# Seven products for half of the state space's output product and for a third gate/up pair

## The chip, the cores and the metric

One core of a Trainium2 chip runs the kernel. The metric is the device time of one execution in microseconds (us); lower is better. Engines are named as in the profile: PE (TensorE matmuls), PEld (its weight loads, which run beside them), DVE (VectorE), ACT (ScalarE), POOL (GpSimd) and SP (SyncE, which issues most loads). L12 is line 12 of the kernel.

## What is computed

Two layers of a decoder trunk on 256 tokens of width 1024, in float32. In each layer, after an RMSNorm, one wide input product feeds a retention mixer and a state-space mixer; each has its own output product, the two results are gated and added, and `w_o` brings them back. A SwiGLU block follows. Only the lines that matter here:

```
    ys = (ysg.reshape(bsz, s, SSD_INNER) * ssd_norm_w.astype(jnp.float32)).astype(h.dtype)
    o_ssd = ys @ ssd_out                                   # (256 x 2048) @ (2048 x 1024)
    merged = jax.nn.sigmoid(gate_ret) * o_ret + jax.nn.sigmoid(gate_ssd) * o_ssd
    return merged @ w_o
...
    gu = h @ w_gate_up                                     # (256 x 1024) @ (1024 x 5632)
    gate, up = jnp.split(gu, [D_FF], axis=-1)
    return (jax.nn.silu(gate) * up) @ w_down               # (256 x 2816) @ (2816 x 1024)
```

## The kernel before, in words

**Precision.** Every float32 operand is split into two float32r parts, high (`wh`) and low (`wl`). A product of 128 rows by 512 columns is three matmuls: high by high, low by high, high by low (`mm3`, L535 to L538). A weight piece is 128 by 1024 numbers (512 KB): SP loads it into a `raw` slot (4 of them), ACT writes `wh` (L499), DVE subtracts to get `wl` (L520). `split_piece` takes one of `HB` = 6 slots for the pair (`hlS`); the matmuls that use it last give it back. Pieces are split in the order in which the products use them (`turn`).

**Three ways to do a product.** *Plain* (`tm_job`, `out_job`): four tiles of 128 tokens by 512 columns. For a gate/up pair of 512 columns each this is 96 matmuls of 512 columns and 8 split pieces. *Feature-major* (`fm_job`, L957 to L960): the weights are stationary, high and low tokens stand side by side, so that a step is one matmul of 512 columns and one of 256; a pair has eight blocks of eight steps and 8 pieces. Its result comes out transposed, as the down product wants it; two PSUM halves have to be added (`gathered`). *Seven products* (`sevens`, `wino_sums`, `seven`): Strassen's scheme in Winograd's form. Tokens and the inner dimension are halved, the pair's two column blocks are the other halves, and seven block products (named 11, t1, t2, 22, t3, 21, t4) of 12 matmuls each take the place of eight: 84 matmuls of 512 columns. For that, the weights have sums: t1 = 11 + 12 and t2 are added by DVE in place (two pieces each), t3 and t4 by a DMA that adds while it writes (`accum_op`, issued by POOL, four in all), and all seven sums have to be split: 14 pieces. The operands have sums too (`seven_sums`: on each of four sums one DVE addition, an ACT copy and a DVE subtraction), and four DVE operations put the products together.

**Buffers of a seven.** The two pieces of 11, which become t1, t2 and t4 in place, lie in the slots of `seg`; those of 12, which become t3, in the two `cc` slots; 22 and 21 in `raw`.

**Where each stands.** In every layer: the mixer's input products (one pair by sevens), `ret`, four jobs `z`, `ssd` (plain, 16 pieces), `wo`, then the feed-forward block `FFN`: pair 0 plain, 1 feature-major, 2 seven, 3 feature-major, 4 seven, and half a pair (index 5) feature-major. The down product (`out_wino`) does 1024 of its 2816 rows (parts 1 and 2 of its operand `gu`) by sevens, mixed into 14 plain pieces by the pattern `AMID`, where "*" is a plain piece and the last five pieces stand behind the pattern.

**What sets the order.** A planner inside the kernel (`Flow`) plays the streams with costs of its own and writes down each engine's instructions in the order that comes out; the engines then run them in that order and wait on semaphores. SP's loads stand in the order of the products' pieces (`feeder`), each behind a free slot.

## Time and profile before

| | |
|---|---|
| median of 3 runs | 1263.66 us (1262.74 to 1264.23) |
| the profiled execution | 1261.89 us, span of its instructions 1260.1 us |
| PE busy | 1251.6 us, 99% of the span, 6330 matmuls |
| DVE busy | 1017.9 us, 81% |
| ACT busy | 832.7 us, 66% |
| POOL busy | 52.6 us, 4% |
| DMA | 253.96 MB, 202 GB/s on average |

A row's "mean ns of one" is longer than the step from one instruction to the next, since neighbours overlap in their pipelines; the step is read from two starts in the timeline. "Idle before" names what ended the wait.

### The profile page before, as it was taken

The numbers are of one execution on the slowest core, as the hardware profiler recorded it, in microseconds if no ns is written. First come the engines' busy times: TensorE is split into PE (matmuls) and PEld (weight loads), VectorE is DVE, ScalarE is ACT, GpSimd is POOL, SyncE is SP. The second block draws the span as 40 slices with busy tenths as digits, with TensorE's granted clock in tenths as the row PEclk, the third lists the DMA queues.
The fourth block names the chain that finished last, engine by engine and source line by source line (L and its number), as shares of the span: only waits on it lengthen the run. The fifth ranks groups of instructions, "written<-read, shape, count | busy, mean of one in ns | idle before, by whom it ended". The sixth has DMA issues, their size and how long they took to land.

```text
span 1260.1 us, 17460 instructions
## 1 busy us (share of the span) xinstructions
PE 1251.6 (99%) x6330; PEld 1061.8 (84%) x6330; DVE 1017.9 (81%) x1388; ACT 832.7 (66%) x1245; POOL 52.6 (4%) x76
## 2 busy tenths in 40 slices
PE   9999999999999999999999999999999999999997
PEld 8889888888888888888888898888888888888886
DVE  6998978878575678999788888878875756888996
ACT  6866786987365466776586676967954643766754
POOL 0000000000010001001000000000000000010010
PEclk9999999999999999999999999999999999999999
DMA  8768555556465557987777475555555664678873
GB/s 298 226 175 276 189 168 174 166 194 196 155 218 201 163 174 224 294 228 206 225 217 220 123 260 175 172 186 169 189 193 176 201 207 151 211 217 257 281 190 114
DMA packets 72456, 253.96 MB, mean 202 GB/s; under 512 B 8337, under 2 KB 8593, under 8 KB 72369
## 3 DMA queue, kind: packets, MB, share of 16 engines
q1 hardware_dynamic: 66832, 233.32, 55.8%
q0 software_dynamic: 5248, 18.99, 7.9%
q8 instruction: 50, 0.82, 0.3%
q10 hardware_dynamic: 288, 0.52, 0.1%
q14 instruction: 38, 0.30, 0.1%
HBM read 251.69 MB, written 1.11 MB: 201 GB/s over the span
## 4 chain that ended last, share of the span: by engine, by line
PE 95%; DVE 2%; DMA 1%; issue 1%; ACT 0%; POOLq 0%; POOL 0%; ACTq 0%
PE acc L536 20%; PE acc L537 20%; PE acc L538 20%; PE acc L957 16%; PE acc L958 9%; PE tr L633 2%; PE acc L960 2%; PE yps L1616 2%; DVE wl L520 1%; DMA raw<-in_w_dw_dram 1%; PE tr L1509 1%; PE acc L1376 1%; PE ips L1603 1%; PE idle L1949 0%; PE y L537 0%
## 5 line engine op out<-in xcount | busy, mean ns | idle before, releaser
L520 DVE TENSOR_TENSOR wl<-raw,wh 128x1024 fp32r<-128x1024 f32 (+2 forms) x400 | 475.4, 1197 | 111.1 <-ACT wh L499 108.9
L499 ACT ACTIVATE wh<-raw 128x1024 fp32r<-128x1024 f32 (+2 forms) x400 | 409.5, 1037 | 214.8 <-PE acc L538 108.7
L957 PE MATMUL acc<-xT,wh 128*128 128x512 f32 x840 | 304.2, 400 | 0.0
L958 PE MATMUL acc<-xT,wl 128*128 128x256 f32 x960 | 252.7, 282 | 0.0
L536 PE MATMUL acc<-wh,xT 128*128 128x512 f32 (+1 forms) x568 | 219.7, 387 | 0.0
L538 PE MATMUL acc<-wh,xT 128*128 128x512 f32 (+1 forms) x568 | 216.3, 381 | 0.0
L537 PE MATMUL acc<-wl,xT 128*128 128x512 f32 (+1 forms) x568 | 216.2, 381 | 0.0
L958 PEld LDWEIGHTS acc<-xT,wl 128*128 128x128 f32 x960 | 181.7, 189 | 10.0
L957 PEld LDWEIGHTS acc<-xT,wh 128*128 128x128 f32 x840 | 158.3, 188 | 32.1
L537 PEld LDWEIGHTS acc<-wl,xT 128*128 128x128 f32 x568 | 106.8, 188 | 20.0 <-issue 1.0
L536 PEld LDWEIGHTS acc<-wh,xT 128*128 128x128 f32 x568 | 106.8, 188 | 19.5 <-issue 1.4
L538 PEld LDWEIGHTS acc<-wh,xT 128*128 128x128 f32 x568 | 106.8, 188 | 19.4
L499 ACT ACTIVATE wh<-raws 128x1024 fp32r<-128x1024 f32 x64 | 67.2, 1056 | 29.7 <-DVE raws L228 14.5
L520 DVE TENSOR_TENSOR wl<-raws,wh 128x1024 fp32r<-128x1024 f32 x64 | 77.4, 1222 | 9.3 <-ACT wh L499 9.1
L231 DVE SCALAR_TENSOR_TENSOR cc<-cc,cv 128x255 f32<-128x255 f32 (+1 forms) x144 | 68.9, 480 | 11.5 <-ACT cc L221 10.4
L536 PE MATMUL acc<-wh,A 128*128 128x512 f32 x192 | 76.4, 398 | 0.0
L538 PE MATMUL acc<-wh,A 128*128 128x512 f32 x192 | 74.9, 390 | 0.0
L537 PE MATMUL acc<-wl,A 128*128 128x512 f32 x192 | 74.8, 390 | 0.0
L536 PE MATMUL acc<-wh,C 128*128 128x512 f32 (+1 forms) x184 | 72.3, 393 | 0.0
L537 PE MATMUL acc<-wl,C 128*128 128x512 f32 (+1 forms) x184 | 71.0, 386 | 0.0
L538 PE MATMUL acc<-wh,C 128*128 128x512 f32 (+1 forms) x184 | 70.8, 385 | 0.0
L536 PE MATMUL acc<-wh,Y 128*128 128x512 f32 x160 | 64.3, 402 | 0.0
(176 smaller groups left out, 1853.4 us busy)
## 6 DMA issues: line engine op xcount, KB each, us to landing
raw<-in_w_tm_dram SPq DMA_DIRECT2D x104, 512.0 KB, 4.3
raw<-in_w_fm_dram SPq DMA_DIRECT2D x80, 512.0 KB, 4.2
raw<-in_w_gf_dram SPq DMA_DIRECT2D x40, 512.0 KB, 4.8
raw<-in_ret_out_dram SPq DMA_DIRECT2D x32, 512.0 KB, 3.9
raw<-in_ssd_out_dram SPq DMA_DIRECT2D x32, 512.0 KB, 3.4
raw<-in_w_gate_up_dram SPq DMA_DIRECT2D x32, 512.0 KB, 5.4
raw<-in_w_down_dram SPq DMA_DIRECT2D x28, 512.0 KB, 4.5
raw<-in_w_gr_dram SPq DMA_DIRECT2D x24, 352.0 KB, 3.9
```

What stands on the lines that cost most here:

```text
L231: return Op("dve", 1.04 * n + 130, lambda: nc.vector.scalar_tensor_tensor(out=out, in0=in0, scalar=scalar, in1=in1, op0=op0, op1=op1), pr)
L499: nc.scalar.activation(out=wh[:, :m], in_=raw[:, :m], func=AF.Copy)
L520: nc.vector.tensor_tensor(out=wl[:, :m], in0=raw[:, :m], in1=wh[:, :m].bitcast(F32), op=ALU.subtract)
L536: nc.tensor.matmul(ps, lhsT=lh, rhs=rh, start=first, stop=False, **kw)
L537: nc.tensor.matmul(ps, lhsT=lh, rhs=rl, start=False, stop=False, **kw)
L538: nc.tensor.matmul(ps, lhsT=ll, rhs=rh, start=False, stop=last, **kw)
L633: nc.tensor.transpose(out=ps[:, j * P : (j + 1) * P], in_=src[:, j * P : (j + 1) * P], identity=ident)
L957: nc.tensor.matmul(a, lhsT=wh[:, k % 4, fsl], rhs=x[:, k % 4, :, :], start=k == 0, stop=False)
L958: nc.tensor.matmul(a[:, :SEQ], lhsT=wl[:, k % 4, fsl], rhs=xh[:, k % 4, :], start=False, stop=False)
L960: nc.tensor.matmul(a, lhsT=wh[:, k % 4, fsl], rhs=x[:, k % 4, :, :], start=False, stop=True)
L1376: nc.tensor.matmul(ps[:, :SEQ], lhsT=k[:, b, :P], rhs=q[:, b, :], start=b == 0, stop=b == 1)
L1616: nc.tensor.matmul(ps[:, i * HD : (i + 1) * HD], lhsT=sg[:, i, :], rhs=xdt[:, i * HD : (i + 1) * HD], start=True, stop=True)
```

## The change

- **Output product of the state space.** Its first 1024 rows (parts 0 and 1 of the operand `yz`) go by sevens, the other 1024 stay plain (8 pieces): `out_wino` is used here too, with a pattern `SMID` of its own, a new weight layout `w_sw`, and `add_m`, which gates the seven's results and adds them to the sum `sgr`. The operand's sums start with job `z` 2.
- **Feed-forward.** Pair 1 goes by sevens in place of feature-major, pair 2 feature-major in place of sevens; pair 3 goes by sevens, and the half pair 5 moves ahead of pair 4, which stays seven and is now last. So three pairs go by sevens and one and a half feature-major.
- **Down product.** In `AMID` six plain pieces, where there were four, stand ahead of the first product; the count is the same.
- **Slots.** `HB` 7 for 6: a seventh pair of `wh` and `wl`. `dynamic_dma_scratch_size` is set to 8192, half of what it was.
- **`seven_sums`** waits for all four parts of its operand before it takes buffers.

```diff
-GF = (1, 3, NPAIR)
+GF = (2, NPAIR)
...
-    HB, RB, TAIL, WARM = 6, 4, 5, 2
+    HB, RB, TAIL, WARM = 7, 4, 5, 2
...
+    ZS_PR = 0.5
...
-    AMID = ("*", "*", "*", "*", "11", "*", "t1", "*", "t2", "22", "*", "t3", "*", "21", "*", "t4")
+    AMID = ("*", "*", "*", "*", "*", "*", "11", "*", "t1", "*", "t2", "22", "*", "t3", "21", "t4")
+
+    SMID = ("*", "*", "11", "*", "t1", "*", "t2", "22", "*", "t3", "21", "t4")
...
         for n in range(2):
             for t in range(NT):
+                yield (plain[n][t] if plain else op.ready[parts[n]][t])
+        for n in range(2):
+            for t in range(NT):
                 if plain:
                     x[n, t] = yield plain[n][t]
                 else:
-                    yield op.ready[parts[n]][t]
...
     FFN = [[("plain", 0)],
-           [("fm", 1)],
-           [("seven", (2,), ("t3", "t4"))],
-           [("fm", 3)],
-           [("seven", (4,), ("t3", "t4"))],
-           [("fm", NPAIR)]]
+           [("seven", (1,), ("t3", "t4"))],
+           [("fm", 2)],
+           [("seven", (3,), ("t3", "t4"))],
+           [("fm", NPAIR)],
+           [("seven", (4,), ("t3", "t4"))]]
...
-            if isinstance(m, tuple):
+            if m == ("ssd",):
+                group(sevens(w_sw[l, 0], w_sw[l, 1], added=("t3", "t4"), order=SMID, slots=(ccS, new_cc)),
+                      plain((out_srcs(ssd_out[l])[8:], ())))
+            elif isinstance(m, tuple):
...
+            if g == 2:
+                fl.spawn(seven_sums(zops, yz, (0, 1), "A", at_job[0] + ZS_PR))
             return tm_job(xT, z_post(g))
...
+        def add_m(t, n, u, j):
+            nsl = slice(n * 512, (n + 1) * 512)
+            yield sgs_ev[t][n]
+            yield mr_ev[t][n]
+            inner = (t, n) == (1, 0)
+            if inner:
+                yield sxS
+            to = new_sx() if inner else u
+            yield tt(512, j, to, u, sgs[t][:, nsl], ALU.mult)
+            yield tt(512, j, sgr[t][:, nsl], sgr[t][:, nsl], to, ALU.add)
+            if inner:
+                fl.release(sxS)
+
+        zops = {q: Event() for q in ALONE}
...
-            return out_job(yz, 16, ssd_post)
+            return out_wino(yz, 16, 0, "A", SMID, ssd_post, add_m, zops)
...
+    out["w_sw"] = cols(a["ssd_out"][:, :1024], [0, 512], 512, 2)
...
-    nc = _bacc.Bacc("TRN2", target_bir_lowering=False, num_devices=1)
+    nc = _bacc.Bacc("TRN2", target_bir_lowering=False, num_devices=1, dynamic_dma_scratch_size=8192)
```

How the instructions stand before and after, at three places. DVE in layer 1, around the end of the plain pair 0. `wl` is a split's subtraction, `raws<-raws,cc` and `raws<-raws,raw` are the additions of t1 and t2, `plain` and `D` the operand's sums. Before:

```order
L520 TENSOR_TENSOR wl<-raw,wh 128x1024
L228 TENSOR_TENSOR D<-plain,D 128x4x128
L520 TENSOR_TENSOR wl<-raw,wh 128x1024
L228 TENSOR_TENSOR plain<-plain 128x512
L520 TENSOR_TENSOR wl<-raw,wh 128x1024
L228 TENSOR_TENSOR D<-plain,D 128x4x128
L520 TENSOR_TENSOR wl<-raw,wh 128x1024
L228 TENSOR_TENSOR plain<-plain 128x512
L520 TENSOR_TENSOR wl<-raw,wh 128x1024 x2
L228 TENSOR_TENSOR D<-plain,D 128x4x128
L228 TENSOR_TENSOR sil<-acc,sil 128x512 x2
```

After, up to the second t2 piece:

```order
L523 TENSOR_TENSOR wl<-raws,wh 128x1024
L229 TENSOR_TENSOR D<-plain,D 128x4x128
L523 TENSOR_TENSOR wl<-raws,wh 128x1024
L229 TENSOR_TENSOR plain<-plain 128x512
L229 TENSOR_TENSOR raws<-raws,cc 128x1024
L229 TENSOR_TENSOR D<-plain,D 128x4x128
L229 TENSOR_TENSOR raws<-raws,raw 128x1024
L229 TENSOR_TENSOR sil<-acc,sil 128x512 x2
L523 TENSOR_TENSOR wl<-raws,wh 128x1024 x2
L229 TENSOR_TENSOR raws<-raws,raw 128x1024
L229 TENSOR_TENSOR A<-tr,A 128x4x128 x2
L523 TENSOR_TENSOR wl<-raw,wh 128x1024
```

In the place of plain splits for a feature-major pair there are now the additions and splits of a seven, among the operand's sums. SP's loads from `wo` to the down product. Before:

```order
L481 DMA raw<-in_w_o_dram 128x1024 x8
L481 DMA raw<-in_w_gate_up_dram 128x1024 x8
L481 DMA raw<-in_w_gf_dram 128x1024 x8
L481 DMA raws<-in_w_gate_up_dram 128x1024 x2
L481 DMA cc<-in_w_gate_up_dram 128x1024 x2
L481 DMA raw<-in_w_gate_up_dram 128x1024 x4
L481 DMA raw<-in_w_gf_dram 128x1024 x8
```

After:

```order
L484 DMA raw<-in_w_o_dram 128x1024 x8
L484 DMA raw<-in_w_gate_up_dram 128x1024 x8
L484 DMA raws<-in_w_gate_up_dram 128x1024 x2
L484 DMA cc<-in_w_gate_up_dram 128x1024 x2
L484 DMA raw<-in_w_gate_up_dram 128x1024 x4
L484 DMA raw<-in_w_gf_dram 128x1024 x8
```

The first seven's eight loads now stand directly behind the eight of the plain pair. POOL between the state space's norm weights and the down product (`rz` and `rstd` are small powers for norms). Before:

```order
L661 DMA wb<-in_norm_ffn_w_dram 128x1024
L241 TENSOR_TENSOR rstd<-ms,mhalf 128x1 x2
L409 DMA cc<-in_w_gate_up_dram 128x1024 x2
L409 DMA raws<-in_w_gate_up_dram 128x1024 x2
L409 DMA cc<-in_w_gate_up_dram 128x1024 x2
L409 DMA raws<-in_w_gate_up_dram 128x1024 x2
L661 DMA wb<-in_norm_mix_w_dram 128x1024
```

After:

```order
L412 DMA cc<-in_w_sw_dram 128x1024
L242 TENSOR_TENSOR rz<-ms,mhalf 128x1
L412 DMA cc<-in_w_sw_dram 128x1024
L242 TENSOR_TENSOR rz<-ms,mhalf 128x1
L664 DMA wb<-in_norm_ffn_w_dram 128x1024
L412 DMA raws<-in_w_sw_dram 128x1024 x2
L242 TENSOR_TENSOR rstd<-ms,mhalf 128x1 x2
L412 DMA cc<-in_w_gate_up_dram 128x1024 x2
L412 DMA raws<-in_w_gate_up_dram 128x1024 x2
```

Adding DMAs stand now between the norm powers of the last `z` job, and there is one more group of four in the feed-forward block. Over the whole program PE has 16 transposes, 144 matmuls of 512 columns more in the plain form (L536 to L538) and 128 fewer of each size in the feature-major form; DVE has 40 operations of 1024 columns (24 splits, 16 additions) and 52 of 512 more, and 16 of 256 fewer; ACT 24 splits more; POOL 16 adding DMAs more (28 before); SP as many loads as before.

## Rows read from the trace of the kernel before

**Rows 1.** The page of the profile: the span, the engines' busy time, PE's share and granted clock in 40 slices, and the first line of the chain that ended last.

```profile
span 1260.1 us, 17460 instructions
PE 1251.6 (99%) x6330; PEld 1061.8 (84%) x6330; DVE 1017.9 (81%) x1388; ACT 832.7 (66%) x1245; POOL 52.6 (4%) x76
...
PE   9999999999999999999999999999999999999997
...
PEclk9999999999999999999999999999999999999999
...
PE 95%; DVE 2%; DMA 1%; issue 1%; ACT 0%; POOLq 0%; POOL 0%; ACTq 0%
```

**Rows 2.** Busy time of each engine in stretches of 10 us of layer 1's feed-forward block; the last two columns are the DMA engines' busy share and GB/s.

```profile
core 0: us, PE busy (x) PEld busy (x) DVE busy (x) ACT busy (x) POOL busy (x), PEclk, DMA share, GB/s
480.00:490.00 10.00, 10.00 (x60) 8.72 (x59) 6.59 (x9) 5.69 (x8) 0.00 (x0) 1.00 0.88 354
490.00:500.00 10.00, 10.00 (x57) 8.64 (x56) 10.00 (x12) 6.50 (x10) 1.80 (x2) 1.00 0.63 106
500.00:510.00 10.00, 10.00 (x45) 8.29 (x45) 10.00 (x12) 8.79 (x11) 1.72 (x2) 1.00 0.80 184
510.00:520.00 10.00, 10.00 (x49) 8.37 (x48) 10.00 (x13) 7.93 (x10) 0.00 (x0) 1.00 0.78 250
...
540.00:550.00 10.00, 10.00 (x47) 8.35 (x46) 10.00 (x12) 8.95 (x11) 2.28 (x3) 1.00 0.74 135
```

**Rows 3.** Timeline of PE in layer 1, from the feature-major pair 1 to the seven of pair 2 and into pair 3 (start in us, busy us, line, operation).

```profile
484.58 0.40 PE L957 MATMUL acc<-xT,wh 128*128 128x512 f32 x1
...
498.68 0.40 PE L536 MATMUL acc<-wh,xT 128*128 128x512 f32 x1
...
501.42 0.39 PE L536 MATMUL acc<-wh,D 128*128 128x512 f32 x1
...
512.30 0.39 PE L536 MATMUL acc<-wh,xT 128*128 128x512 f32 x1
```

**Rows 4.** The chain of waits, one step of it: PE's eight transposes of two tiles.

```profile
458.88 0.87 PE tr L633 x8
```

**Rows 5.** Timeline of DVE through the seven of pair 2 in layer 1; a bracket, where there is one, is idle time ahead of the row.

```profile
500.33 1.22 DVE L520 TENSOR_TENSOR wl<-raws,wh 128x1024 fp32r<-128x1024 f32 x1
...
502.07 2.36 DVE L520 TENSOR_TENSOR wl<-raw,wh 128x1024 fp32r<-128x1024 f32 x2
504.34 0.69 DVE L228 TENSOR_TENSOR C<-sil,C 128x512 fp32r<-128x512 f32 x1
504.94 2.36 DVE L520 TENSOR_TENSOR wl<-cc,wh 128x1024 fp32r<-128x1024 f32 x2
507.22 1.22 DVE L520 TENSOR_TENSOR wl<-raw,wh 128x1024 fp32r<-128x1024 f32 x1
```

**Rows 6.** Timeline of DVE in layer 1 behind the norm, during the plain pair 0, and in the feature-major pair 1.

```profile
464.54 2.35 DVE L520 TENSOR_TENSOR wl<-raw,wh 128x1024 fp32r<-128x1024 f32 x2
...
478.98 0.69 DVE L228 TENSOR_TENSOR A<-tr,A 128x512 fp32r<-128x512 f32 x1 [0.37 <-ACT A L221]
479.58 0.41 DVE L228 TENSOR_TENSOR sil<-acc,sil 128x256 f32<-128x256 f32 x1
479.91 0.68 DVE L228 TENSOR_TENSOR A<-tr,A 128x512 fp32r<-128x512 f32 x1
481.58 1.22 DVE L520 TENSOR_TENSOR wl<-raw,wh 128x1024 fp32r<-128x1024 f32 x1 [0.98 <-ACT wh L499]
```

**Rows 7.** Busy time of each engine over layer 1's feed-forward block up to the down product; columns as in rows 2.

```profile
452.00:572.00 120.00, 120.00 (x619) 102.28 (x617) 108.91 (x129) 87.21 (x117) 8.06 (x10) 1.00 0.81 248
```

**Rows 8.** Timeline of PE in layer 1: the first matmul of the plain pair 0.

```profile
452.59 0.39 PE L536 MATMUL acc<-wh,xT 128*128 128x512 f32 x1
```

**Rows 9.** Timeline of SP's loads in layer 1: those of the plain pair 0, then of pair 1.

```profile
433.88 22.32 SPq L481 DMA_DIRECT2D raw<-in_w_gate_up_dram  x8
457.35 11.64 SPq L481 DMA_DIRECT2D raw<-in_w_gf_dram  x5
```

**Rows 10.** The page's DMA issues: operation, count, KB each, median us from issue to landing.

```profile
raws<-in_w_gate_up_dram SPq DMA_DIRECT2D x8, 512.0 KB, 7.0
cc<-in_w_gate_up_dram SPq DMA_DIRECT2D x8, 512.0 KB, 8.6
raws<-in_w_gate_up_dram POOLq DMA_DIRECT2D x8, 512.0 KB, 6.7
```

**Rows 11.** Timelines of POOL and of ACT in layer 1's first feed-forward seven: the second adding DMA of t4, and the split of the piece that it makes.

```profile
502.08 0.86 POOL L409 DMA_DIRECT2D raws<-in_w_gate_up_dram  x1 [0.84 <-PE acc L538]
...
510.22 1.06 ACT L499 ACTIVATE wh<-raws 128x1024 fp32r<-128x1024 f32 x1 [0.66 <-DVE wl L520]
```

**Rows 12.** All instructions of L409, the adding DMAs that POOL issues (from the answer on that line: durations in ns, then the time to landing).

```profile
L409 POOL DMA_DIRECT2D raws<-in_w_gate_up_dram x8: 854/860/868, 500.4 to 1167.7; - x8
DMA to landing us min/median/max: 5.2/5.5/9.7
```

**Rows 13.** Timeline of DVE in layer 1 during the plain output product of the state space.

```profile
396.60 1.23 DVE L520 TENSOR_TENSOR wl<-raw,wh 128x1024 fp32r<-128x1024 f32 x1 [1.49 <-ACT wh L499]
399.32 1.23 DVE L520 TENSOR_TENSOR wl<-raw,wh 128x1024 fp32r<-128x1024 f32 x1 [1.50 <-ACT wh L499]
```

More of the change, by code (lines that the diff above doesn't have):

```diff
@@ L1881, in add_h @@
             yield tt(512, j, h[t][:, nsl], h[t][:, nsl], u, ALU.add)
-        yield from out_wino(gu, FF // P, DW, "D", AMID, add_to(nxt), add_h)
+        ops = {q: Event() for q in ALONE}
+        fl.spawn(seven_sums(ops, gu, (DW, DW + 1), "D", at_job[0] - 1.2))
+        yield from out_wino(gu, FF // P, DW, "D", AMID, add_to(nxt), add_h, ops)
     def rotary_half(rotary, dst, which, done):
```

9 lines of the change are left out of this document (4 added, 5 removed).

## The prediction

> **What bounds the kernel now.** I read the page first: PE is busy for 1251.6 of 1260.1 us, no slice but the last is under nine tenths, the granted clock is at its upper level of 2.4 GHz in every slice, and PE holds 95% of the chain that ended last [rows 1]. So the sum of PE's steps is the time, and an edit is worth the steps it takes out as long as PE doesn't begin to wait. Who would make it wait is read from the stretches of 10 us: in the feed-forward sevens DVE is busy 10.00 of 10 us while PE is busy 10.00 as well [rows 2]. DVE is full there and just in time; ACT has room. Last I read steps from the timelines: 48 matmuls of 512 columns take 512.30 - 501.42 = 10.88 us, 0.2267 us each, and five feature-major blocks 498.68 - 484.58 = 14.10 us, 2.82 each [rows 3]; eight transposes put 0.87 us on the chain [rows 4].
>
> **The change part by part.** *State space's output product.* Eight block products become seven: 12 matmuls fewer, 12 x 0.2267 = 2.72 us per layer. *Third pair by sevens.* A feature-major pair is eight blocks, 22.56 us; a seven is 84 x 0.2267 = 19.04 us, and its result needs 8 transposes, 0.87: 19.91. That is 2.65 us less per layer. In all PE loses 2 x (2.72 + 2.65) = 10.74 us. Swapping pairs 1 to 3, the order of `AMID` and the new layouts on the host add no PE step.
>
> *What DVE gets.* Back to back, a step of 1024 columns is 1.135 us (504.34 - 502.07 for two), one of 512 is 0.60 [rows 5], one of 256 is 0.33 (479.91 - 479.58) [rows 6]. A seven asks DVE for 14 splits, 4 additions and 8 steps of 512: 20.4 + 4.8 = 25.2 us beside 19.9 of PE. A feature-major pair asks for 8 splits, 8 steps of 256 and 4 of 512: 14.1 us beside 22.6. So a seven overruns by 5.3 us and lives on work done ahead; a feature-major pair leaves 8.5, the half pair 4.2. The third seven puts 11.1 us more on DVE where 108.91 of 120.00 us are busy [rows 7].
>
> I therefore add up DVE's new order in layer 1, from a row both orders share: the split at 464.54 [rows 6], after which the new order has, up to the second split of t2, 8 splits, 4 additions and 9 steps of 512: 19.0 us, done at 483.6. PE starts pair 0 at 452.59 [rows 8]; 96 matmuls and eight transposes later, at 475.2, the first seven begins; with products 11 and t1, eight transposes of pair 0's result and half of t2, that piece is due at 482.9. It is 0.7 us late. In the kernel before, the same piece of the first feed-forward seven was done at 500.33 + 1.13 = 501.5 [rows 5] and due at 498.68 [rows 3] + 5.44 + 1.36 = 505.5, four early. Further along: the second seven's piece comes after 55.7 us of steps, at 520.2, due about 526; the third's after 88.3 us, at 552.9, due about 557; the down product's after 132.2 us, at 596.7, due about 599. Those margins hold only without DVE idling in between, and waits of 0.3 to 1 us for ACT or a load stand in the same block now [rows 6]. In exchange the seventh slot lets a split go one piece earlier, and six plain pieces of 2.72 us of PE and 1.135 of DVE now stand ahead of the down's seven.
>
> *First seven's loads.* They follow directly behind pair 0's, so SP issues them from 457.35 on, where pair 1's went [rows 9]. The second `cc` load goes out at about 459.2 and lands 8.6 us later [rows 10], at 467.8; the first t1 addition is due in DVE's order at 467.4. At most half a us.
>
> *Adding DMAs.* In the first seven t2's second split ends at 483.6. From the issue of t4's second adding DMA to the split of that piece, 510.22 - 502.08 = 8.1 us pass now [rows 11], with 0.6 ahead of the issue and 2.3 for ACT and DVE behind it: 494.6, due at about 494.5 with the delay above. On the edge. POOL itself needs 0.86 us for each [rows 12] and is otherwise idle.
>
> *State space seven on DVE.* DVE gets 14 splits and 4 additions for 8 splits, 12 steps for the operand's sums and 10 for adding: 10 x 1.135 + 22 x 0.60 = 24.6 us. DVE now idles 1.5 of every 2.72 us in that product [rows 13], 24 us over 16 pieces, and the sums fall into the last two `z` jobs. I cost it at nothing: its first weight sum is wanted after four products of 2.72 us, and its POOL work is the same four issues. If that cover is gone, the price is the 5.3 us overrun of a seven per layer.
>
> *Seventh slot, halved scratch.* The slot costs no instruction. What scratch POOL's transfers need, no row shows. At the least nothing changes; at the most only one adding DMA is in flight, and t4's second waits for the first: some 2 us in each first seven, 4 us in all. I take nothing, since two in flight is the most that any product asks for.
>
> *Sum.* PE -10.74. Waits: 0.7 late split plus a late load or DMA, 1 us per layer in the first seven, and half a us where the down's margin of 2 us meets DVE's idle: 3.0 us for both layers; bounds 0 and twice 5.3 = 10.6, if the seven that has no feature-major pair ahead of it pays its whole overrun. 1261.89 - 10.74 + 3.0 = 1254.15 for the profiled execution; the median of the three runs is 1.77 above it: **1255.9 us**. The opening and the closing chain behind the last matmul are untouched.
>
> **The rivals.**
>
> *A. DVE becomes the bound (the other side).* Place: the feed-forward block, from pair 0 to the down product. For it: DVE is full in sevens already [rows 2], works in order, and a late piece delays all behind it. Of 120.00 us, 11.1 are idle now [rows 7]. If this idle time is waiting for results, not for slots, it stays: 108.9 + 11.1 (new work) + 11.1 = 131.1 us, less 3 pieces of the down product that need not be split by then (3.4), 127.7, against 117.4 of PE: 10.3 us per layer, 20.6 in all, 1273.5. It decides from 6.6 us per layer on: then the waits exceed 10.74 by 2.5, a measurable loss. With half the price it ends at 1263, no change. Against it: the longest idle times stand in feature-major stretches (6.59 of 10 us busy at 480 to 490 [rows 2]), just where splits are ahead and wait for a slot, and a seventh is added. 0.17: 0.08 slower, 0.05 no change, 0.04 faster.
>
> *B. Adding DMAs land late.* The slowest adding DMA took 9.7 us where 5.5 is the median [rows 12]. If those of t4 in the first sevens do, 4.2 us more fall on each, since that chain has no margin: 1255.9 + 8.4 = 1264.3; if only half, 1260. For it: 16 more such DMAs, and the DMA engines' share is 0.81 in this block [rows 7]. Against it: from t2's split to t4's use lie four products. The Trainium skill has a rule in this direction: in "SBUF — State Buffer", section "Who interferes with whom", a DMA that GpSimd issues can starve for its descriptors while DVE holds the port pair that the two share, in a two-port mode. By that rule a block with DVE at 100% would land such DMAs late throughout, which is this rival's price and no other. The trace doesn't bear it out so far: with DVE at 10.00 of 10 us each issue took 0.854 to 0.868 us [rows 2, 12]. 0.10: 0.06 faster, 0.04 no change.
>
> *C. No waits at all.* DVE's margins hold, and the seventh slot makes up the first seven's 0.7: 1255.9 - 3.0 = 1252.9. Faster, 0.08.
>
> That the change doesn't take out what it says is excluded: the built order has 144 matmuls of 512 columns more and 128 of each size fewer. 144 x 0.2267 + 1.74 - 16 x 2.82 = -10.74, the same sum.
>
> **How the numbers follow.** Forecast 0.65, rivals 0.17, 0.10 and 0.08. About 0.2%, 2.5 us, is what a measurement of this kernel can tell from no change, so faster means under 1261.1 and slower over 1266.2. Faster: 0.65 + 0.04 + 0.06 + 0.08 = 0.83; same 0.05 + 0.04 = 0.09; slower 0.08. The forecast's own range is 1253 to 1259. The range reaches down past rival C by a us and up to 1261.5, into the half prices of A and B; what lies above has some 0.15, below 0.04.
>
> **What would show it.** In the changed profile PE should have busy time of about 1241 us, still 99% of a span near 1252, and splits (`wl`) should end the few idle times ahead of it. Right: in layer 1's state-space product no idle time of PE; in the first feed-forward seven a wait of about a us at t2 or t4; DVE at 10 of 10 us from pair 0 into the down product. Wrong, towards A: idle PE ahead of the second and third seven or in the down product, released by `wl`, with DVE never idle. Towards B: ACT's split of `raws` or `cc` waiting for a gate/up DMA. If PE's steps themselves change (a pitch other than 0.2267, a lower granted clock), the sum itself is wrong.

## The result, and the profile after

The changed kernel takes 1265.38 us (median of 21 runs, 1262.87 to 1267.87); the kernel before, on the same chips, 1262.94 us (21 runs, 1261.95 to 1264.87). The ratio is 1.0019, its 95% interval 1.0012 to 1.0025: 2.4 us slower. The forecast was 1255.9 us, with a range from a us below 1252.9 up to 1261.5, so the time lies above it, and it moved the other way. The profiled execution took 1267.58 us, 2.2 above the median; before's took 1261.89, 1.1 below its median. So the two profiled executions differ by 5.7 us (5.5 between their spans), and where that matters below, medians decide.

From the page after: span, engines, and the first line of the chain that ended last.

```profile
span 1265.6 us, 17387 instructions
...
PE 1246.9 (99%) x6234; PEld 1049.6 (83%) x6234; DVE 1082.8 (86%) x1464; ACT 856.8 (68%) x1273; POOL 73.6 (6%) x92
...
PE 35%; DVE 7%; DMA 3%; issue 2%; ACT 1%; POOL 0%; POOLq 0%; SPq 0%; ACTq 0%; DVEq 0%
```

PE's busy time fell by 4.7 us, not by 10.74. Of the missing 6 us, 1.7 are a lower clock, shown at the end; the rest is time that the profile counts as busy although PE stood (a matmul's end is modelled, so a wait is listed shorter than it is, 0.37 for two starts 0.76 us apart at 485.28, and a short one not at all). PE's idle time rose from 8.5 to 18.7 us, DVE's busy time by 64.9, and PE's share of the chain went from 95% [rows 1] to 35%: the end now hangs on what PE waits for. The waits of PE in the kernel before (us in total, times, longest):

```profile
PE idle L1949 <- DVE mhalf L1926: 1.3, 1, 1.3
PE acc L537 <- DVE wl L520: 0.2, 1, 0.2
```

The same view of after:

```profile
PE acc L539 <- ACT sx L222: 3.6, 3, 2.6
PE tr L636 <- DVE D L229: 2.8, 2, 1.4
PE idle L1975 <- DVE mhalf L1952: 1.3, 1, 1.3
PE tr L636 <- DVE sil L229: 1.3, 2, 0.7
PE acc L540 <- DVE wl L523: 1.1, 3, 0.4
PE cps L1547 <- ACT D L222: 0.7, 1, 0.7
PE acc L1383 <- DVE C L229: 0.5, 1, 0.5
PE tr L636 <- DVE sil L232: 0.2, 1, 0.2
```

The first line is copies of a PSUM bank in the sevens, the second the transposes behind the state space's seven, the fourth those of a seven's result, the sixth and seventh the first layer's mixer, which the change doesn't touch. The fifth are late splits: 0.37 us in each layer's first seven, 0.35 in layer 1's down product.

**Where the time went.** Read from PE's timeline: the start of the first matmul of each stage, and the difference to the next stage's. Stages that aren't shown (the retention product, the `z` jobs, layer 2's mixer) agree within 0.3 us in all kernels. Where three pairs go by sevens, the last seven's eight transposes (0.87 us [rows 4]) stand behind the first matmuls of the down product: PE has 16 transposes there and 8 before, so that 3.52 us of steps leave a block, 0.87 come to a down product, and 2.65 are gone from both. S is the stretch from the start to layer 1's retention product, "ssd" the state space's product with `wo`, "FFN" pair 0 to the down product, "down" the down product up to layer 2's first matmul; the last one runs to the end of the span. All in us.

| kernel | S | ssd 1 | FFN 1 | down 1 | ssd 2 | FFN 2 | down 2 |
|---|---|---|---|---|---|---|---|
| before | 283.36 | 69.11 | 119.76 | 58.42 | 69.10 | 119.76 | 65.04 |
| after | 285.93 | 68.08 | 119.81 | 60.28 | 68.00 | 122.57 | 65.16 |
| scratch_only | 283.72 | 69.10 | 119.76 | 58.47 | 69.12 | 119.76 | 64.65 |
| slots_only | 284.92 | 69.11 | 119.72 | 58.11 | 69.11 | 119.72 | 64.49 |
| six_slots | 284.53 | 68.03 | 118.43 | 62.52 | 68.17 | 119.23 | 67.98 |
| ssd_only | 285.55 | 68.09 | 119.75 | 58.10 | 67.91 | 119.79 | 64.19 |
| ssd_six | 283.30 | 67.99 | 119.76 | 58.44 | 67.67 | 119.76 | 64.78 |
| ssd_t1dma | 285.32 | 68.16 | 119.76 | 58.10 | 67.79 | 119.75 | 64.20 |
| ssd_no_sums | 284.97 | 66.46 | 119.76 | 58.10 | 66.55 | 119.76 | 64.29 |
| ssd_tail | 285.39 | 73.20 | 117.41 | 60.63 | 71.31 | 120.76 | 65.51 |
| ssd_mid | 284.57 | 68.92 | 119.76 | 58.44 | 69.07 | 119.79 | 64.97 |
| ssd_slack | 286.80 | 69.15 | 119.72 | 58.10 | 69.08 | 119.75 | 64.25 |
| ssd_six_slack | 283.64 | 69.04 | 119.76 | 58.43 | 69.02 | 119.78 | 64.90 |
| ffn_only | 286.34 | 69.12 | 118.52 | 60.00 | 69.11 | 119.10 | 65.25 |
| amid_old | 285.71 | 67.91 | 118.99 | 61.95 | 67.88 | 120.39 | 68.93 |
| t4_dve | 284.87 | 68.06 | 117.45 | 64.12 | 68.39 | 118.80 | 69.12 |
| ffn_t1dma | 285.87 | 67.98 | 132.76 | 61.48 | 68.17 | 136.50 | 66.18 |
| ffn_no_t1 | 285.75 | 67.72 | 116.92 | 59.98 | 67.99 | 116.91 | 65.16 |
| t1_pool | 285.60 | 67.94 | 125.38 | 60.05 | 67.95 | 125.26 | 65.17 |
| t1_pool_six | 284.22 | 67.98 | 120.96 | 63.52 | 67.77 | 123.47 | 67.59 |

In after, S grew by 2.57, the two ssd stages shrank by 2.13 where 5.44 of matmuls left them, and feed-forward block and down product grew by 4.84 where 5.30 left them. The other stages add 0.2, in all 5.5 us of span.

**DVE in the state space's product**, 40 us of it, before (sum and mean of four windows of 10 us, 384 to 424):

```profile
sum 40.00, PE 40.00 PEld 33.21 DVE 21.86 ACT 15.81 POOL 1.64; mean PE 10.00 PEld 8.30 DVE 5.46 ACT 3.95 POOL 0.41
```

And after, 386 to 426:

```profile
sum 40.00, PE 39.30 PEld 32.20 DVE 38.89 ACT 26.26 POOL 6.56; mean PE 9.82 PEld 8.05 DVE 9.72 ACT 6.56 POOL 1.64
```

The half-idle DVE of this product is gone, and at its end PE waits for it: PE's timeline after (start, busy us; in brackets the wait ahead).

```profile
424.91 0.39 PE L541 MATMUL acc<-wh,C 128*128 128x512 f32 x1
426.72 0.63 PE L636 MATMUL tr<-cst,D 128*128 128x128 f32 x4 [1.42 <-DVE D L229]
```

**The feed-forward blocks** after, one window for each layer; the row of before and the columns are in [rows 7]:

```profile
454.00:574.00 120.00, 117.90 (x575) 97.88 (x574) 115.02 (x131) 85.26 (x114) 11.51 (x14) 1.00 0.82 246
1078.00:1200.00 122.00, 118.55 (x572) 98.38 (x571) 116.24 (x133) 86.74 (x115) 11.51 (x14) 0.99 0.83 246
```

DVE went from 108.91 to 115.02 of 120 us. The largest wait is in layer 2's last seven. POOL's timeline there, with t4's second adding DMA:

```profile
1181.57 0.87 POOL L412 DMA_DIRECT2D raws<-in_w_gate_up_dram  x1 [0.60 <-DVE wl L523]
```

ACT's:

```profile
1191.11 1.06 ACT L502 ACTIVATE wh<-raws 128x1024 fp32r<-128x1024 f32 x1 [3.16 <-DMA raws<-in_w_gate_up_dram]
1192.08 1.04 ACT L502 ACTIVATE wh<-raw 128x1024 fp32r<-128x1024 f32 x1
1194.40 1.06 ACT L502 ACTIVATE wh<-raw 128x1024 fp32r<-128x1024 f32 x1 [1.28 <-DMA raw<-in_w_down_dram]
1195.37 0.58 ACT L222 ACTIVATE sx<-acc 128x512 f32<-128x512 f32 x1
```

And PE's:

```profile
1193.05 0.39 PE L541 MATMUL acc<-wh,xT 128*128 128x512 f32 x1
1196.00 0.57 PE L539 MATMUL acc<-wh,xT 128*128 128x512 f32 x1 [2.56 <-ACT sx L222]
1196.36 0.63 PE L540 MATMUL acc<-wl,xT 128*128 128x512 f32 x1
...
1199.75 0.39 PE L539 MATMUL acc<-wh,xT 128*128 128x512 f32 x1
```

DVE splits t2 late, so POOL issues t4's second adding DMA late; it is used 9.5 us later (1191.11 - 1181.57), and ACT stands before it in its fixed order. Behind that stand two splits of the down product's pieces, and behind those the copy of the bank that PE needs. The second of these splits waits another 1.28 us, for its own load. SP issued that one at

```profile
1184.82 0.33 SPq L484 DMA_DIRECT2D raw<-in_w_down_dram  x1
```

directly behind DVE's split of 1183.54, and it was used 9.6 us later. So the wait that ends last is this load: in ACT's order the copy would have stood at 1195.37 with the adding DMA on time, too, as long as the load landed when it did. The same chain costs 0.83 us in layer 1, and there too a down load ends it (ACT waits 0.89 us for it at 569.54).

### The profile page after: what moved, and what is told of

Read it like the earlier page. It is cut to its first block, busy times and chain, and to the rows that moved or that the text cites. A ratio compares the mean times of both kernels' runs of the same rounds, so it can differ in the third digit from the quotient of the medians.

```text
span 1265.6 us, 17387 instructions
## 1 busy us (share of the span) xinstructions
PE 1246.9 (99%) x6234; PEld 1049.6 (83%) x6234; DVE 1082.8 (86%) x1464; ACT 856.8 (68%) x1273; POOL 73.6 (6%) x92
## 5 line engine op out<-in xcount | busy, mean ns | idle before, releaser
L523 DVE TENSOR_TENSOR wl<-raw,wh 128x1024 fp32r<-128x1024 f32 (+2 forms) x384 | 454.2, 1193 | 70.8 <-ACT wh L502 68.7
L962 PE MATMUL acc<-xT,wh 128*128 128x512 f32 x728 | 263.0, 399 | 0.0
L539 PE MATMUL acc<-wh,xT 128*128 128x512 f32 (+1 forms) x592 | 229.9, 388 | 3.6 <-ACT sx L222 3.6
L541 PE MATMUL acc<-wh,xT 128*128 128x512 f32 (+1 forms) x592 | 226.1, 382 | 0.0
L963 PE MATMUL acc<-xT,wl 128*128 128x256 f32 x832 | 218.5, 281 | 0.0
L963 PEld LDWEIGHTS acc<-xT,wl 128*128 128x128 f32 x832 | 157.0, 189 | 8.6
L962 PEld LDWEIGHTS acc<-xT,wh 128*128 128x128 f32 x728 | 136.9, 188 | 28.2
L502 ACT ACTIVATE wh<-raws 128x1024 fp32r<-128x1024 f32 x96 | 101.4, 1059 | 70.0 <-DVE raws L229 34.5
L523 DVE TENSOR_TENSOR wl<-raws,wh 128x1024 fp32r<-128x1024 f32 x96 | 115.9, 1217 | 8.4 <-ACT wh L502 8.0
L539 PE MATMUL acc<-wh,A 128*128 128x512 f32 x224 | 89.4, 399 | 0.0
L541 PE MATMUL acc<-wh,A 128*128 128x512 f32 x224 | 87.4, 390 | 0.0
L540 PE MATMUL acc<-wl,D 128*128 128x512 f32 x128 | 50.1, 391 | 0.7 <-DVE wl L523 0.7
```

What stands on the lines that cost most here:

```text
L502: nc.scalar.activation(out=wh[:, :m], in_=raw[:, :m], func=AF.Copy)
L523: nc.vector.tensor_tensor(out=wl[:, :m], in0=raw[:, :m], in1=wh[:, :m].bitcast(F32), op=ALU.subtract)
L539: nc.tensor.matmul(ps, lhsT=lh, rhs=rh, start=first, stop=False, **kw)
L540: nc.tensor.matmul(ps, lhsT=lh, rhs=rl, start=False, stop=False, **kw)
L541: nc.tensor.matmul(ps, lhsT=ll, rhs=rh, start=False, stop=last, **kw)
L962: nc.tensor.matmul(a, lhsT=wh[:, k % 4, fsl], rhs=x[:, k % 4, :, :], start=k == 0, stop=False)
```

## The experiments

Ratios are to the kernel before on the same chip, with their 95% intervals. Of the diffs only the core is shown.

### Each part alone

**slots_only**, the kernel before with seven slots and half the scratch, and **scratch_only**, with the latter alone:

```diff
-    HB, RB, TAIL, WARM = 6, 4, 5, 2
+    HB, RB, TAIL, WARM = 7, 4, 5, 2
...
-    nc = _bacc.Bacc("TRN2", target_bir_lowering=False, num_devices=1)
+    nc = _bacc.Bacc("TRN2", target_bir_lowering=False, num_devices=1, dynamic_dma_scratch_size=8192)
```

> The kernel before with seven slots and the halved scratch, nothing else. Theory W: within 0.5 us of before, and the first layer's mixer as before. Rival R: 2 to 3 us slower, with PE waits between 90 and 200 us in the first layer's mixer that before doesn't have, or with adding DMAs whose landing takes longer than 5.5 us in the median.

> The kernel before with the halved scratch alone: every engine's order is that of before. As predicted: no change, 1262.3 to 1263.3. Rival: the 1.2 us of the kernel with seven slots and halved scratch are the scratch's: 1263.5 to 1264.5, adding DMAs landing later than 5.5 us in the median.

1263.93 us, ratio 1.0008 (1.0000 to 1.0017), and 1262.89 us, ratio 1.0001 (0.9992 to 1.0010). The scratch costs nothing that shows. The slots change an order: from some 45 us on, in the first layer, the planner writes another one for PE, DVE, ACT and SP, the same in all kernels with seven slots up to the last `z` jobs. S is 284.87 to 286.80 us in the 13 kernels that have it (mean 285.6) and 283.30 to 284.57 in the seven that keep six slots and before's order (mean 283.9): 1.7 us, where single traces with the same order differ by up to 1.9. slots_only gains 0.3 and 0.55 us of it back in the down products, so some 0.9 us is left; its median lies 1.2 above before's, between theory W (0.5) and rival R (2 to 3).

**ssd_only**: the changed kernel with `FFN`, `GF` and `AMID` as before. **ffn_only**: the changed kernel with the state space's product plain (the operand's sums and the weights' group for it undone too). The core of both:

```diff
-           [("seven", (1,), ("t3", "t4"))],
-           [("fm", 2)],
-           [("seven", (3,), ("t3", "t4"))],
-           [("fm", NPAIR)],
-           [("seven", (4,), ("t3", "t4"))]]
+           [("fm", 1)],
+           [("seven", (2,), ("t3", "t4"))],
+           [("fm", 3)],
+           [("seven", (4,), ("t3", "t4"))],
+           [("fm", NPAIR)]]
...
-            return out_wino(yz, 16, 0, "A", SMID, ssd_post, add_m, zops)
+            return out_job(yz, 16, ssd_post)
```

> The changed kernel with the feed-forward block and the down product as before (pairs 2 and 4 by sevens, four plain pieces ahead of the down's seven); the state space's seven, seven slots and the halved scratch stay. Theory W (the waits are made locally, by the work that each new seven brings): in the profile of after the state space's product and wo took 1.03 and 1.10 us less than before in place of 2.72, so 1262.9 - 2.1 = about 1261, with the wait ahead of the first transposes (1.4 us, DVE) still in each layer. Rival R (slots or scratch reorder or delay the whole program, the 2.6 us in the first layer's mixer among it): about 1263.5. Rival N (the state space's seven costs nothing on DVE, as predicted): 1257.5.

> The changed kernel with the state space's output product plain as before; the third feed-forward seven, the new AMID, seven slots and the halved scratch stay. Theory W: feed-forward block and down product took 1.91 us more than before in layer 1 and some 2.9 more in layer 2 in the profile of after (an execution 2.2 us above the median), so 1265 to 1267. Rival R: most of the loss is the slots' or the scratch's, so this is above before by them, 1266 or more, and the kernel with slots and scratch alone shows it. Rival N (all the loss is the state space's): about 1258.

1261.02 us, ratio 0.9990 (0.9981 to 0.9998), and 1266.25 us, ratio 1.0030 (1.0018 to 1.0042), as theory W has both. So the sign comes from the feed-forward part: over slots_only the state space's seven wins 0.0018 (2.3 us), the third pair loses 0.0022 (2.8 us).

### The state space's seven

**ssd_t1dma**: as ssd_only, t1's sums by adding DMAs.

```diff
-                group(sevens(w_sw[l, 0], w_sw[l, 1], added=("t3", "t4"), order=SMID, slots=(ccS, new_cc)),
+                group(sevens(w_sw[l, 0], w_sw[l, 1], added=("t1", "t3", "t4"), order=SMID, slots=(ccS, new_cc)),
```

> The kernel with the state space's seven alone (1261.0 us), in which t1's two weight sums are made by adding DMAs too, so that DVE has two additions of 1024 columns less, 2.27 us a layer; POOL has two more DMAs. Theory D (DVE has more work than the product lasts, and the excess falls on the last additions ahead of the transposes): the wait of 1.4 us ahead of these transposes goes in both layers, 1261.0 - 2.9 = 1258. Rival L (it is the latency of the chain behind the last product, whatever DVE did before): the wait stays at 1.3 to 1.5 us, 1261. Rival B (the two more adding DMAs land late): 1263 or more, with waits for wl at t1 or t2.

1261.21 us, ratio 0.9986 (0.9978 to 0.9995). Theory D missed, and rival L (the latency of the chain behind the last product) had the number: the waits stayed at 1.43 and 1.07 us. The planner now set the first transposes three matmuls earlier into PE's order, so a part of DVE's lead was spent before it could show.

**ssd_no_sums**: as ssd_only, without the additions of t1 and t2 in that seven.

```diff
+            elif bare:
+                yield raw
             else:
                 w = yield raw
                 yield tt(D, pr, x, x, w, ALU.add)
```

> The kernel with the state space's seven alone and seven slots (1261.0 us), in which that seven leaves out the additions that make t1 and t2 (its products then use 11's pieces again): 4.5 us less on DVE in each layer's product, the waits for the loads stay. Theory D (DVE's load, of which 2.3 us less was not enough): the wait ahead of the first transposes falls below 0.5 us in both layers and the stage from this product to the feed-forward block to 66.4 to 66.9 us from 68.1 and 67.9: 1258 to 1259. Rival L (the chain behind the last product, over the loads of w_o and ACT's splits of them, sets it): the wait stays at 1.2 to 1.5 us, 1261.

1258.41 us, ratio 0.9962 (0.9949 to 0.9976). The stage takes 66.46 and 66.55 us: 2.65 and 2.55 less than before, nearly the whole 2.72. The waits of PE:

```profile
PE idle L1977 <- DVE mhalf L1954: 1.3, 1, 1.3
PE tr L638 <- DVE sil L232: 0.8, 2, 0.5
PE acc L1385 <- DVE C L229: 0.4, 1, 0.4
```

The line of transposes waiting for `D` is gone, though they stand three matmuls earlier here, too, so rival L falls. It is DVE's load, and 2.3 us less of it isn't enough. (Why that bought nothing at all is settled only as far as the order of the transposes goes.)

**ssd_tail** and **ssd_mid**: five and four plain pieces behind the seven where three were; ssd_tail from the changed kernel, ssd_mid from ssd_only with six slots.

```diff
-    SMID = ("*", "*", "11", "*", "t1", "*", "t2", "22", "*", "t3", "21", "t4")
+    SMID = ("*", "11", "*", "t1", "*", "t2", "22", "t3", "21", "t4")
...
+    SMID = ("*", "*", "11", "*", "t1", "*", "t2", "22", "t3", "21", "t4")
```

> The changed kernel with two plain pieces of the state space's product moved from SMID behind its seven (five behind it, where three were). Theory W (DVE has not added the seven's results by the time the first transpose of the gated sum is due; three plain pieces give it 8.2 us): the waits of 1.4 us ahead of these transposes go in both layers, 1265.4 - 2.8 = 1262.6. Rival P (the wait is paid earlier instead, since the seven's pieces come closer together and DVE's splits are late for them): 1264.5 to 1266, with waits for wl inside the product.

> The kernel with the state space's seven alone, six slots and the full scratch (1261.1 us), with one plain piece moved behind the seven: four behind it, where three were (five were slower by 4 us in the changed kernel). Theory D: DVE has 2.7 us more until the transposes, so their waits of 1.0 and 0.8 us go, and the pieces of t3 to t4 lose less than that: 1259 to 1260.5. Rival P (the seven's own splits come late, as with five behind it): waits for wl inside the product, 1262 or more.

1269.60 us, ratio 1.0057 (1.0044 to 1.0069), and 1263.89 us, ratio 1.0006 (0.9998 to 1.0015). Rival P's mechanism both times: waits for `D` go, waits for `wl` (4.6 us in all in ssd_tail, 1.9 in ssd_mid) and one of 1.8 us for `wh` in ssd_tail take their place. Moving the pieces moves the place of a debt. ssd_tail is 3.6 us over P's range (1264.5 to 1266), and its trace has a lower clock: 0.59 and less from 419 to 426 us, 0.67 and less from 1047 to 1051, some 5.1 us of the 8.4 by which its two product stages are longer than after's. ssd_mid has no lower clock there.

**ssd_slack** (from ssd_only) and **ssd_six_slack** (the same with six slots, full scratch):

```diff
-            yield from transposed(sgr[t][:, nsl], 4, mT, n, t, j - 1)
+            yield from transposed(sgr[t][:, nsl], 4, mT, n, t, j - 1, slack=SLOW)
```

> The kernel with the state space's seven alone (1261.0 us), its planner told to place the transposes of the gated sum 1.5 us later among PE's matmuls, nothing else. Theory E (DVE, full to the end of this product, runs behind the planner's times, and PE's fixed order has the transposes ahead of matmuls that could run): the wait of 1.3 to 1.5 us ahead of them goes in both layers, 1261.0 - 2.5 = 1258.5. Rival G (the lateness is only passed on, to the first matmuls of w_o, whose operand these transposes make): 1260.5 to 1261.5, with a wait there.

> The same kernel with later transposes, six slots and the full scratch: no seventh slot. With six slots every engine's order up to the last z jobs of layer 1 is that of before. Theory S (the seventh slot costs some 1.5 us there, and the state space's seven and the old feed-forward block need only six): from the start to the retention product 283.4 to 284.5 us in place of 285.5, and the rest unchanged: 1.5 us below the kernel with seven slots and later transposes. Rival F (the slot is needed for the product's 14 splits): the state space's stage loses over 1 us a layer, with waits for wl, and the sum is no gain.

1266.53 us, ratio 1.0033 (1.0022 to 1.0045), and 1263.35 us, ratio 1.0006 (0.9997 to 1.0015). Theory E falls: the wait turns up in `wo`, as rival G has it, but longer, and ssd_slack's time lies 5 us above G's range. Its trace, the fastest of its six executions, shows 3.4 us over ssd_only's. PE's timeline in ssd_slack:

```profile
430.60 0.39 PE L540 MATMUL acc<-wl,A 128*128 128x512 f32 x1
432.74 0.50 PE L541 MATMUL acc<-wh,A 128*128 128x512 f32 x1 [1.75 <-DVE A L229]
```

**ssd_six**: ssd_only with six slots and the full scratch.

```diff
-    HB, RB, TAIL, WARM = 7, 4, 5, 2
+    HB, RB, TAIL, WARM = 6, 4, 5, 2
```

> The kernel with the state space's seven alone (1261.0 us with seven slots), with six slots and the full scratch and the transposes where they were. Theory S: 1.8 us less from the start to the first retention product, the state space's stage at 68.1 as with seven: 1259 to 1259.5. Rival F: that stage loses what the mixer gains, 1261.

1261.07 us, ratio 0.9987 (0.9978 to 0.9996). S is back at 283.30 us and the product loses nothing with six slots. The median doesn't show the 2 us of S (0.9990 with seven), so the slot's price in the medians isn't settled: ssd_only and ssd_six show 0.4 us, slots_only and scratch_only 1 us, ssd_slack and ssd_six_slack 3. This kernel beats both the one before and the changed one, by 0.13% and some 0.3%.

### The third feed-forward seven

The five kernels here, with their edits in the order ffn_no_t1, t1_pool, ffn_t1dma (the same for pair 4) and t4_dve. **ffn_no_t1**: the changed kernel without the additions of t1 in the second and third feed-forward seven. **t1_pool**: these additions done by POOL. **t1_pool_six**: that with six slots and the full scratch. **ffn_t1dma**: done by adding DMAs. **t4_dve**: t4's sums in the last seven by DVE, not DMA.

```diff
+        if bare:
+            yield w12
+            fl.set(used["t1"])
+        else:
             yield from plus("t1", x, w12, "12")
...
-                yield tt(D, pr, x, x, w, ALU.add)
+                yield (pool if q in aside else tt)(D, pr, x, x, w, ALU.add)
...
-           [("seven", (3,), ("t3", "t4"))],
+           [("seven", (3,), ("t1", "t3", "t4"))],
...
-           [("seven", (4,), ("t3", "t4"))]]
+           [("seven", (4,), ("t3",))]]
```

> The changed kernel, in which the second and third feed-forward sevens leave out the two additions that make t1 (the product is then done with 11's pieces once more): 4.5 us less on DVE in each layer's block, as with the adding DMAs for t1, but without their transfers. Theory A (DVE's load is what PE waits for): the waits ahead of the second seven's transposes and in the down product go, and stage times approach the plain sum (feed-forward block 117.1, down product 58.1): 1259 to 1261.5. Theory B (the adding DMAs of t4 and ACT's queue behind them): the waits for ACT's copy in the last seven stay at 0.6 to 2.6 us, and only the others go: 1263 to 1264.5.

1258.40 us, ratio 0.9969 (0.9957 to 0.9981), a little below theory A's range. Both blocks take 116.9 us, 2.85 less than before, of the 3.52 us of steps that leave them. Block and down product together take 4.0 us less than before, the two layers added (5.30 worked out), so 1.3 us of loss are left where after has 10.1. The waits of PE, the same view as of after:

```profile
PE tr L640 <- DVE D L229: 2.4, 2, 1.3
PE acc L544 <- DVE wl L527: 1.5, 4, 0.5
PE idle L1979 <- DVE mhalf L1956: 1.3, 1, 1.3
PE tr L640 <- DVE sil L232: 1.0, 2, 0.8
PE acc L1387 <- DVE C L229: 0.5, 1, 0.5
```

The line `ACT sx` is gone with it: the late adding DMA and the late down load were DVE's lateness passed on, at least in part (see t4_dve). After's additions of t1 had no idle time ahead of them in those two sevens (DVE's timeline, 513.88 to 516.8 and 546.76 to 549.1), so what the kernel saves is load, not a wait.

> The changed kernel, in which the last feed-forward seven makes t4's two weight sums by DVE additions in place of adding DMAs (2.3 us more on DVE, two adding DMAs less). Theory B (the waits of 0.8 and 2.6 us in that seven come from t4's adding DMA, 9 us on its way, behind whose split ACT's copy of a PSUM bank is queued): these waits go or fall below 0.3 us, 1263 to 1264. Theory A (DVE has no room there): t4's split and the down product's come later by as much as DVE has more to do, 1265.5 to 1268, with waits for wl.

1269.62 us, ratio 1.0054 (1.0041 to 1.0066). Both theories are half right: no wait for the bank's copy is left, and the blocks shrink to 117.45 and 118.80, but the down products grow to 64.12 and 69.12, waiting for `wl` (6.9 us in all, some in the sevens). DVE is no earlier here; but the first two down loads landed 3.2 to 4.4 us after their issue, where after's took 6.9 to 9.5 beside the adding DMAs. So the wait in the last seven took both: a late DVE and slow transfers. 2.3 us more on DVE cost more than the two DMAs did.

> The changed kernel, in which the second and the third feed-forward seven make t1's two weight sums by adding DMAs too: 4.5 us less on DVE in each layer's block. Theory A (DVE's load is what PE waits for in this block): the waits ahead of the second seven's transposes (0.7 and 0.5 us) and those in the down product (0.5 to 0.7) go, and that at the last seven shrinks: 1262 to 1263.5. Theory B (the late transfers are it): four more adding DMAs in a block whose DMA engines are 0.8 busy, 1266 to 1269.

1297.19 us, ratio 1.0271 (1.0257 to 1.0285), far beyond either theory. In the kernel of the state space plain pieces stand between 11 and t1; here nothing does, so each chain of split, DMA and split lies open. Landing of the adding DMAs, and the longest of ACT's waits for one. The first, from the answer on L412, the line of all adding DMAs:

```profile
DMA to landing us min/median/max: 5.2/7.3/12.9
```

ACT's timeline:

```profile
567.16 2.00 ACT L502 ACTIVATE wh<-raws 128x1024 fp32r<-128x1024 f32 x2 [5.37 <-DMA raws<-in_w_gate_up_dram]
```

> The changed kernel, in which the second and third feed-forward sevens have t1's two additions done by POOL in place of DVE: the same 4.5 us less on DVE in each layer's block as in the kernel that leaves them out, but the additions, and the waits for their loads, stay. Theory A (DVE's load alone): both feed-forward blocks near 117 us and no wait for ACT's copy in the last seven, 1258.5 to 1260. Rival K (what helped in the kernel without t1's additions was that its pieces no longer waited for 12's load): the blocks stay at 119 to 122, 1264 to 1266. Rival Q (POOL's addition of 1024 columns takes so long, or slows DVE beside it so much, that t1 is late): waits for wl or wh at t1, 1263 or more.

> The same with six slots and the full scratch. Theory S (the seventh slot costs 1.8 us in the first layer's mixer; the sevens need it only because DVE runs late): start to retention product 283.4 to 284.5, 1.5 us below the kernel with seven: 1257 to 1258.5. Rival F (the down product needs it anyhow: with six slots it took 62.5 us in place of 60.3): 1260 to 1262.

1275.30 us, ratio 1.0101 (1.0087 to 1.0115), and 1273.25 us, ratio 1.0081 (1.0067 to 1.0094). Rival Q: the blocks take 125.4 and 125.3 us, waiting for copies behind late splits of t1 and t2 (up to 3.6 us at one place, with a lower clock behind it in both layers, some 3.4 us); the last section shows the two engines beside each other. Six slots change the size, not the sign.

**six_slots** (the changed kernel, `HB` 6 as above) and **amid_old** (its `AMID` as before):

```diff
-    AMID = ("*", "*", "*", "*", "*", "*", "11", "*", "t1", "*", "t2", "22", "*", "t3", "21", "t4")
+    AMID = ("*", "*", "*", "*", "11", "*", "t1", "*", "t2", "22", "*", "t3", "*", "21", "*", "t4")
```

> The changed kernel with six slots for split pieces in place of seven; the halved scratch stays. Theory S (the planner, given a seventh slot, writes another order for the first layer's mixer, which is slower by some 2 us there, and the sevens hardly use the slot): the time from the start to the first layer's retention product falls from 285.9 to about 283.4 us, 1265.4 - 2.5 = 1263. Rival F (the sevens of the state space and the feed-forward block live on the seventh slot): that stretch gains the same, but the later ones lose more, with waits for wl: 1266 to 1269. If that stretch stays at 285 or more with six slots, the slot isn't its cause.

> The changed kernel with the down product's old pattern AMID (four plain pieces ahead of its seven, not six). Theory A (DVE enters the down product in arrears, and the six plain pieces let it catch up): more waits for wl in the down product, 1266.5 to 1269. Rival M (the new pattern, which has the last products with hardly a plain piece between, is what makes the down product 1.6 to 1.9 us longer in layer 1): 1263 to 1264.5.

1266.53 us, ratio 1.0030 (1.0021 to 1.0039, which overlaps after's interval), and 1267.83 us, ratio 1.0045 (1.0033 to 1.0057). Theory S holds for S (284.53) and fails for the sum: with three feed-forward sevens the down product needs the slot (62.52 and 67.98 us). And theory A holds for `AMID`: with four pieces ahead, the plain piece between the down's t1 and t2 waits 1.75 and 1.83 us for its `wl` (and a lower clock behind the latter adds 1.7 us in the trace). Six pieces and a seventh slot pay for debts that the third seven makes.

## Why the prediction was wrong

**PE's steps: right as far as read.** Where DVE is relieved, the product of the state space gains 2.65 and 2.55 (2.72 worked out), feed-forward block and down product together 1.28 in layer 1 and 2.73 in layer 2 (2.65).

**"I cost it at nothing" (state space's seven on DVE): failed.** 24.6 us of new work against 24 us of idle time left no reserve, and the idle time was smaller than the two rows of [rows 13] made it look: over the whole product DVE idled 45.80 - 26.17 = 19.6 us before (columns as in [rows 2]).

```profile
383.50:429.30 45.80, 45.80 (x213) 38.04 (x212) 26.17 (x30) 19.80 (x26) 1.64 (x3) 1.00 0.48 161
```

After, DVE is full to the product's end (38.89 of 40 us). It cost PE 68.08 - 66.46 = 1.62 and 68.00 - 66.55 = 1.45 us of each 2.7, not nothing and not the 5.3 of "if that cover is gone".

**"Waits: ... 3.0 us": failed, the largest piece.** In feed-forward blocks and down products after, the traces show 4.84 + 5.30 = 10.1 us of new loss, 7.1 more than the sum had, near its upper bound of 10.6 (1.7 of it is the lower clock, which that sum had no term for). The ledger for the first seven was right: it put t2's second split at 483.6 on before's clock, 485.2 on after's, where pair 0 starts 1.6 later. DVE's timeline after, that split and the next instruction:

```profile
484.01 1.21 DVE L523 TENSOR_TENSOR wl<-raws,wh 128x1024 fp32r<-128x1024 f32 x1
485.15 1.21 DVE L523 TENSOR_TENSOR wl<-raw,wh 128x1024 fp32r<-128x1024 f32 x1
```

The split's step ends where the next begins, at 485.15, and PE waited 0.37 us for it, in both layers (0.7 late was forecast). No late load came with it, and of the adding DMAs little: t4's second one landed at 493.35, 7.8 us after its issue, and the copy behind ACT's split of it kept PE 0.17 us in layer 1. What failed is the sentence "Those margins hold only without DVE idling in between", and what was made of it: between there and the second seven's t2, DVE idles 2.6 us for ACT's splits (1.10, 0.74, 0.53 and 0.18 us at 494.54, 507.44, 509.53 and 511.26; ahead of the first ACT stood until that adding DMA had landed, ahead of the next two until loads of the feature-major pair had), smaller gaps and steps a little longer than 1.135 and 0.60 add 0.9, and that piece ends at 525.2, not 521.8. The margins of 4 to 6 us still held for the t2 pieces. They didn't for three other things that DVE owes and that I checked nowhere: the second seven's result (0.73 and 0.52 us ahead of its transposes), the copy in the last seven, behind t4's adding DMA and a down load that SP issued late, behind a split of DVE (0.83 and 2.56 us), and the down product of layer 1 (1.0 us of its 1.86 more, since 0.87 are the transposes that moved there; a wait of 0.35 us for `wl` at 622.28 is the largest piece).

**"The slot costs no instruction": right, but "I take nothing" failed.** It changes the planner's order in the first layer's mixer, 1.7 us in the mean of the traces, 2.6 between before's and after's. **Halved scratch: right**, 1.0001.

**Rivals.** A was the right one, at about half its price (4.6 and 5.6 us per layer, from 180.09 - 178.18 + 2.65 and 187.73 - 184.80 + 2.65), and not only in the feed-forward block. Against it I held that DVE idles most in feature-major stretches, where a seventh slot lets it work ahead. The slot does help there (six_slots is 1.1 us slower than after), but the change leaves one such pair fewer, and the argument priced neither. B's mechanism showed, in the last seven more than in the first: the wait there went when DVE was relieved (ffn_no_t1) and also when the last two adding DMAs were left out (t4_dve). The step from a two-port mode to "a block with DVE at 100%" in B's rule is borne out by nothing here: no row tells a mode of DVE, and POOL's issues for the block took 0.859 to 0.887 us in after.

**The sum again, for the profiled spans**: -10.74 for PE, +10.1 feed-forward and down, +3.3 state space, +2.6 first mixer, +0.2 elsewhere: 5.5. The medians are 3.3 us closer to each other than the traces. One part of that is the lower clock: of after's 21 executions, 15 have a mean granted clock of 0.999 and only two, the profiled one among them, 0.997. How long the wait ahead of it is in the others isn't on record; at the same place ffn_only's trace has 0.66 us and no lower clock.

## What to carry to other kernels

When a change trades steps of the bounding engine for steps of one that is already busy nine tenths of a stage, add up that second engine's whole stage, idle times that it cannot use included; if the sum comes within a few per cent of the stage, price the overlap, not nothing. Check every result that the second engine owes (results to be added, issues that wait for it, copies queued behind those), not only its next operands. And a bigger buffer pool isn't free where a planner sets the order: it re-plans stages that the change never meant.

## What the hardware showed beyond that

**DVE and POOL slow each other.** In t1_pool POOL's addition of 1024 columns took 2.40 to 4.51 us. The line of that group (durations in ns, least, median, longest):

```profile
L242 POOL TENSOR_TENSOR raws<-raws,cc x8: 2396/3016/4509, 510.9 to 1178.6; 128x1024 f32<-128x1024 f32 x8
```

DVE's timeline in t1_pool: three rows while POOL adds (510.86 to 516.8), one of them with an input in PSUM (`acc`), and one row after that:

```profile
511.69 0.42 DVE L229 TENSOR_TENSOR sx<-acc,sx 128x256 f32<-128x256 f32 x1
512.14 2.44 DVE L229 TENSOR_TENSOR sil<-sx,sil 128x512 f32<-128x512 f32 x1
515.28 2.12 DVE L229 TENSOR_TENSOR Y<-sil,Y 128x512 fp32r<-128x512 f32 x1 [0.70 <-ACT Y L222]
...
527.89 0.68 DVE L229 TENSOR_TENSOR sil<-sx,sil 128x512 f32<-128x512 f32 x1
```

0.68 us became 2.44 and 2.12 where both inputs lie in SBUF; the step with one input in PSUM kept its 0.42. At another place POOL paid instead: its longest addition, 4.51 us from 545.28 on, began inside a DVE step, and DVE's three with both inputs in SBUF kept their 0.69, 0.69 and 1.23 us. The Trainium skill, "SBUF — State Buffer", section "Who interferes with whom", has this rule: a DVE instruction with two SBUF inputs contends with a GpSimd instruction that reads SBUF. The trace agrees, and with it went the hope to relieve DVE by an engine that is 94% idle: nothing of what ffn_no_t1 wins could be had so.

**Behind a wait of 2.6 us the clock was halved.** Granted clock after the wait of layer 2's last seven (the clock is the third number from the right):

```profile
1195.00:1196.00 1.00, 0.00 (x1) 0.00 (x1) 1.00 (x3) 1.00 (x3) 0.00 (x0) 1.00 0.06 25
1196.00:1197.00 1.00, 1.00 (x3) 0.83 (x4) 1.00 (x2) 0.98 (x2) 0.00 (x0) 0.64 0.85 238
1197.00:1198.00 1.00, 1.00 (x3) 0.78 (x3) 1.00 (x2) 0.96 (x1) 0.00 (x0) 0.50 0.88 303
...
1200.00:1201.00 1.00, 1.00 (x6) 0.83 (x5) 1.00 (x2) 0.36 (x1) 0.00 (x0) 1.00 0.83 315
```

PE went from 2.4 to 1.2 GHz, and nine matmuls took 1199.75 - 1196.00 = 3.75 us where 9 x 0.2267 = 2.04 would do: 1.7 us on top of the wait. Behind the waits of 1.4 us (after), 1.75 us (ssd_slack) and 1.89 us (t1_pool, 527.95) the granted clock stayed at 1.00; behind 1.83 us (amid_old, 1220.84) it fell to 0.50, and so it did in ssd_tail around waits of 1.77 and 1.37 us (419.62 and 1046.64), each with one of 0.76 or 0.78 us ahead of it. So the length of a single wait doesn't tell, in these traces, whether the clock falls.
